# First feed-forward part of a decoder layer: input tiles normed and transposed four at a time, the first weight block split by other engines, the second half's transposes in another place

## The chip, the cores and the metric

The kernel runs on one core of a Trainium2 chip. The time is the device time of one execution in microseconds (us). The engines are PE (TensorE, matrix products), DVE (VectorE), ACT (ScalarE), POOL (GpSimd) and SP (SyncE, which only issues transfers here). Each runs its own row of instructions in order and waits on semaphores for the others.

## The reference

One hybrid decoder layer on x of 1 x 1024 x 1024 in float32. The change concerns the first of its three parts:

```python
x = x + 0.5 * post1(SwiGLU_1(pre1(x)))
# rmsnorm(x, g) = x * rsqrt(mean(x*x) + 1e-6) * g
# swiglu(x)     = (silu(x @ w_gate) * (x @ w_up)) @ w_down     w_gate, w_up: 1024 x 2816
```

Then follow a mixer (stick-breaking attention beside a recurrent head group, between two projections) and a second feed-forward part like the first.

## The kernel before

Every float32 operand of a matrix product is held as two parts, a rounded one (h) and the rest (l), and each product is done as three: h by h, l by h, h by l (`mm3`, lines 119 to 122). `weight` (lines 94 to 110) loads a block of 128 columns of a weight (128 x 1024, 512 KB) into a buffer `wr`, of which there are two, and POOL splits it: line 108 copies it to `wh`, line 109 subtracts for `wl`.

The tokens are worked in two halves of 512. A half's x comes as four tiles of 128 tokens by 1024. Before the change two tiles at a time (`n_00`, `n_01` of the first half, `n_10`, `n_11` of the second) are loaded, squared and summed (ACT line 633, DVE line 768), turned into a factor r by small operations (lines 126 to 137), multiplied by it (ACT line 778, DVE line 780) and given to `to_channels` (line 149). That function transposes on PE (line 159, 128 x 128 each) into a PSUM bank, and from there ACT writes X_0h or X_1h (line 166) and DVE X_0l or X_1l (line 167), channels on partitions. With two tiles a bank holds two blocks of 256 columns, and each is evacuated by itself.

The hidden width has 22 blocks f of 128. Blocks 0 and 1 are plain: `plain_mm(f, h)` does 24 matmuls for the gate (PSUM f1pX) and 24 for the up weight (f1pZ), and `plain_evac` makes silu(gate) * up in a `wr` buffer f1e, splits it and stores it. Blocks 2 to 21 use a form with seven products instead of eight (`product(f)`, in the order 1, 2, 5, 6, 4, 7, 3 into the banks X, Z, DY, X, DW, X, DY, 12 matmuls each). It needs two things: `combine`, sums and differences of X's parts, mostly DVE operations of 128 x 2048 (lines 252 to 267), and `prep(f)`, the same for the raw weights f1r in a scratch f1S of which there is one (DVE lines 303 to 305 and 309), with the split of the seven operands on POOL (lines 314, 315) and ACT (line 312). `load(f)` brings the raw weights, for odd f into the `wr` buffers. `evac1` and `product` read the banks (lines 419 to 449; f1y at line 441, f1v at line 442 and f1u at line 445 are DVE's).

`up` (line 459) runs load(2), combine, plain blocks for the second half, prep(2), and then for each f prep(f+1), load(f+2) and product(f). A scheduler decides the order of each engine's row from the dependencies and its own estimates; the pools decide which buffer must be free first. So the code's order and the rows are not the same, and an edit can move instructions that it does not name.

## Time and profile before

| | us |
|---|---|
| median of 3 runs | 2238.72 |
| lowest and highest | 2233.92, 2238.86 |
| profiled execution | 2238.49 |
| its span, first to last instruction | 2236.7 |
| PE busy | 2106.6 (94%) |
| DVE busy | 1336.3 (60%) |
| POOL busy | 1113.9 (50%) |
| ACT busy | 821.3 (37%) |

PE's mean granted clock is 0.967 of full. The chain that ended last belongs to PE for 76% of the span. A row of the timeline reads: start, duration, engine, line, operation, what it writes and reads, count, and in brackets how long the engine stood idle ahead of it and what released it. Everything that the change names lies in the first 100 us of the 2237.

### The profile page before, as it was taken

What the parts mean: (1) busy time and instruction counts of PE and PEld (TensorE: products, weight loads), DVE (VectorE), ACT (ScalarE), POOL (GpSimd) and SP (SyncE); (2) the same over time, 40 slices, a digit from 0 to 9 for tenths busy, and PEclk for the clock granted to TensorE, in tenths of its full rate; (3) what the DMA queues carried; (4) which work ended last, traced back from release to release, by engine and by line L of the source; (5) the groups of instructions that cost most, each with busy time, mean ns of one, the idle gap of its engine ahead of it and who ended that gap; (6) DMA issues with size and microseconds to landing.
All of it is one profiled execution on the core that took longest, in us unless ns stands there. A gap on an engine that the chain in (4) does not pass through costs nothing.

```text
span 2236.7 us, 30262 instructions
## 1 busy us (share of the span) xinstructions
PE 2106.6 (94%) x10976; PEld 1730.0 (77%) x10976; DVE 1336.3 (60%) x1900; ACT 821.3 (37%) x1429; POOL 1113.9 (50%) x899
## 2 busy tenths in 40 slices
PE   7889999998999999999999999898889999998998
PEld 5668888887888777677888888677668888886886
DVE  5757676742556555735617778636676777733555
ACT  4323333333204534324136657436333333333102
POOL 2676666648742354344311111221687666647734
PEclk8889999999999999999989999999899999998999
DMA  4135555567764463363764673343235554666865
GB/s 123 44 95 165 144 154 149 159 193 282 258 213 132 123 183 119 95 177 98 228 163 118 189 206 115 133 132 131 60 104 158 139 166 131 169 215 212 253 213 188
DMA packets 415476, 353.83 MB, mean 158 GB/s; under 512 B 35168, under 2 KB 337248, under 8 KB 415328
## 3 DMA queue, kind: packets, MB, share of 16 engines
q1 hardware_dynamic: 406800, 347.45, 51.6%
q10 hardware_dynamic: 8528, 4.46, 0.9%
q8 instruction: 87, 1.43, 0.3%
q14 instruction: 61, 0.50, 0.1%
HBM read 224.96 MB, written 126.88 MB: 157 GB/s over the span
## 4 chain that ended last, share of the span: by engine, by line
PE 76%; DVE 9%; issue 4%; POOL 4%; ACT 3%; DMA 2%; SPq 0%; DVEq 0%; POOLq 0%; ACTq 0%
PE pj L120 3%; PE pj L122 3%; PE pj L121 2%; PE f1X L120 2%; PE f2X L120 2%; PE f1X L122 2%; PE f1X L121 2%; PE f2X L122 2%; PE f2X L121 2%; PE f1DY L120 2%; PE f2DY L121 2%; PE f2DY L122 2%; PE f1DY L122 2%; PE f1DY L121 2%; PE f2DY L120 1%
## 5 line engine op out<-in xcount | busy, mean ns | idle before, releaser
L108 POOL TENSOR_SCALAR wh<-wr 128x1024 fp32r<-128x1024 f32 x55 | 62.9, 1145 | 274.6 <-PE wod L122 57.1
L315 POOL TENSOR_TENSOR f1wl<-f1r,f1wh 128x512 fp32r<-128x512 f32 x100 | 139.3, 1406 | 13.0 <-ACT f1wh L312 9.7
L315 POOL TENSOR_TENSOR f2wl<-f2r,f2wh 128x512 fp32r<-128x512 f32 x100 | 139.1, 1404 | 13.0 <-ACT f2wh L312 9.7
L109 POOL TENSOR_TENSOR wl<-wr,wh 128x1024 fp32r<-128x1024 f32 x55 | 137.5, 2503 | 3.2 <-PE pj L122 0.2
L314 POOL TENSOR_SCALAR f1wh<-f1r 128x512 fp32r<-128x512 f32 x60 | 68.0, 1139 | 119.6 <-PE f1pX L121 48.4
L314 POOL TENSOR_SCALAR f2wh<-f2r 128x512 fp32r<-128x512 f32 x60 | 68.0, 1138 | 110.5 <-PE f2pX L121 40.9
L507 DVE TENSOR_TENSOR f2acc<-f2dX,f2acc 128x512 f32<-128x512 f32 x64 | 44.3, 692 | 76.6 <-PE f2dX L122 42.7
L507 DVE TENSOR_TENSOR f1acc<-f1dX,f1acc 128x512 f32<-128x512 f32 x64 | 44.3, 692 | 75.2 <-PE f1dX L122 75.2
L1402 POOL TENSOR_SCALAR a_0B<-a_512B 128x1 f32<-128x1 f32 x32 | 15.4, 481 | 132.0 <-DVE a_512B L1403 98.4
L120 PE MATMUL pj<-x1X4h,wh 128*128 128x512 f32 x176 | 75.5, 429 | 0.5 <-DVE tw L918 0.5
L120 PE MATMUL pj<-x1X2h,wh 128*128 128x512 f32 x176 | 72.1, 409 | 0.6 <-DVE qkl L1113 0.5
L122 PE MATMUL pj<-x1X4h,wl 128*128 128x512 f32 x176 | 71.3, 405 | 0.0
L121 PE MATMUL pj<-x1X4l,wh 128*128 128x512 f32 x176 | 69.7, 396 | 0.0
L122 PE MATMUL pj<-x1X2h,wl 128*128 128x512 f32 x176 | 69.0, 392 | 0.0
L121 PE MATMUL pj<-x1X2l,wh 128*128 128x512 f32 x176 | 68.9, 391 | 0.0
L315 POOL TENSOR_TENSOR f2wl<-f2S,f2wh 128x512 fp32r<-128x512 f32 x40 | 62.3, 1568 | 1.7
L315 POOL TENSOR_TENSOR f1wl<-f1S,f1wh 128x512 fp32r<-128x512 f32 x40 | 62.3, 1568 | 1.7
L533 POOL TENSOR_TENSOR f1dwl<-f1B,f1dwh 128x1024 fp32r<-128x1024 f32 x20 | 47.7, 2412 | 18.9 <-ACT f1dwh L532 18.9
L533 POOL TENSOR_TENSOR f2dwl<-f2B,f2dwh 128x1024 fp32r<-128x1024 f32 x20 | 47.5, 2395 | 19.0 <-ACT f2dwh L532 19.0
L120 PE MATMUL wod<-wh,ymh 128*128 128x512 f32 x128 | 51.1, 399 | 1.1 <-DVE woacc L192 0.9
L122 PE MATMUL wod<-wh,yml 128*128 128x512 f32 x128 | 50.2, 395 | 0.1
L121 PE MATMUL wod<-wl,ymh 128*128 128x512 f32 x128 | 50.1, 392 | 0.0
(1476 smaller groups left out, 7131.6 us busy)
## 6 DMA issues: line engine op xcount, KB each, us to landing
f1ho<-f1hs_d SPq DMA_DIRECT2D x112, 256.0 KB, 4.6
f2ho<-f2hs_d SPq DMA_DIRECT2D x112, 256.0 KB, 4.1
f1hs_d<-f1h SPq DMA_DIRECT2D x56, 256.0 KB, 3.3
f1hs_d<-f1l SPq DMA_DIRECT2D x56, 256.0 KB, 3.0
f2hs_d<-f2h SPq DMA_DIRECT2D x56, 256.0 KB, 3.2
f2hs_d<-f2l SPq DMA_DIRECT2D x56, 256.0 KB, 2.9
wr<-in_w_in_dram SPq DMA_DIRECT2D x27, 512.0 KB, 3.9
f1r<-in_ffn_w_gate_dram SPq DMA_DIRECT2D x19, 512.0 KB, 4.9
```

The source lines that it names most:

```text
L108: nc.gpsimd.tensor_scalar(wh, raw, 1.0, 0.0, op0=ALU.mult, op1=ALU.add)
L109: nc.gpsimd.tensor_tensor(wl, raw, wh, op=ALU.subtract)
L120: nc.tensor.matmul(ps, lhsT=lh, rhs=rh, start=first, stop=False, **kw)
L121: nc.tensor.matmul(ps, lhsT=lh, rhs=rl, start=False, stop=False, **kw)
L122: nc.tensor.matmul(ps, lhsT=ll, rhs=rh, start=False, stop=last, **kw)
L314: nc.gpsimd.tensor_scalar(wh, src[n], 1.0, 0.0, op0=ALU.mult, op1=ALU.add)
L315: nc.gpsimd.tensor_tensor(wl, src[n], wh, op=ALU.subtract)
L507: nc.vector.tensor_tensor(quarter(tt, n), ps, quarter(tt, n), op=ALU.add)
L533: nc.gpsimd.tensor_tensor(wl, src[n], wh, op=ALU.subtract)
L1402: nc.gpsimd.tensor_scalar(B[:, w:w + 1], iv, 1.0, 0.0, op0=ALU.mult, op1=ALU.add)
```

## The change

All four tiles of a half are now loaded by `x_load` and normed together by `x_norm`: one factor r for four tiles, then eight groups of four transposes, each filling a bank of 512 columns that one ACT and one DVE operation evacuate. The first half's banks come from two pools in turn ("D" and "Z"). The gate weight of block 0 is split by ACT (copy) and DVE (subtract) instead of POOL. In the code the second half's loading now stands ahead of both plain blocks, and its norming and transposes between `plain_mm(0, 0)` and `plain_mm(1, 0)`, instead of all of it behind both. The number of matmuls, transposes and warm-up matmuls is the same.

```diff
--- before.py
+++ after.py
@@ -91,7 +91,7 @@
     EX = [None]
     warmt = [None]
 
-    def weight(src, a_, b_, extra=None):
+    def weight(src, a_, b_, extra=None, early=False):
         i = cnt[0]
         cnt[0] += 1
         if extra is None:
@@ -105,8 +105,12 @@
         nc.sync.dma_start(raw, src)
         wh = cut(wp.tile("wh", f"wh{i}", [P, 1024], F32R))
         wl = cut(wp.tile("wl", f"wl{i}", [P, 1024], F32R))
-        nc.gpsimd.tensor_scalar(wh, raw, 1.0, 0.0, op0=ALU.mult, op1=ALU.add)
-        nc.gpsimd.tensor_tensor(wl, raw, wh, op=ALU.subtract)
+        if early:
+            nc.scalar.copy(wh, raw)
+            nc.vector.tensor_tensor(wl, raw, wh, op=ALU.subtract)
+        else:
+            nc.gpsimd.tensor_scalar(wh, raw, 1.0, 0.0, op0=ALU.mult, op1=ALU.add)
+            nc.gpsimd.tensor_tensor(wl, raw, wh, op=ALU.subtract)
         return wh, wl
 
     wz = cp.tile([P, HT], BF16, name="wz")
@@ -327,9 +331,9 @@
             return ps
 
 
-        def plain_load(self, f):
+        def plain_load(self, f, early=False):
             c = slice(f * P, (f + 1) * P)
-            self.op[f] = weight(self.wg[:, :, c], KB, P, False) + weight(self.wu[:, :, c], KB, P, False)
+            self.op[f] = weight(self.wg[:, :, c], KB, P, False, early) + weight(self.wu[:, :, c], KB, P, False)
 
         def plain_mm(self, f, h):
             if f not in self.op:
@@ -753,37 +757,40 @@
     XP[0] = Pool("xp1", XB, "right")
     F1.X = [xpair(f"X1_{h}") for h in range(2)]
     pl = Pool("f1x", dict(t4=8, t2=4))
-    for h in range(2):
-        for p2 in range(2):
-            nm = f"n1_{h}{p2}"
-            xts = []
-            ss = ts(nm + "s", 2)
-            for i in range(2):
-                tt = h * 4 + p2 * 2 + i
-                xt = pl.t4(f"x0_{tt}")
-                nc.sync.dma_start(xt, a["x"][0, tt * P:(tt + 1) * P, :])
-                xts.append(xt)
-                if tt % 2:
-                    junk = pl.t2(f"{nm}j{i}", [P, 1024], BF16)
-                    nc.vector.scalar_tensor_tensor(junk, xt, 1.0, xt, op0=ALU.mult, op1=ALU.mult,
-                                                   accum_out=ss[:, i:i + 1])
-                else:
-                    sumsq_into(pl, f"{nm}q{i}", xt, ss[:, i:i + 1])
-            if h == 0:
-                F1.plain_load(p2)
-            r = rsqrt_col(nm, ss, 1.0 / D, EPS, n=2)
-            for i in range(2):
-                tt = h * 4 + p2 * 2 + i
-                if i == 0:
-                    nc.scalar.activation(xts[i], xts[i], AF.Copy, scale=r[:, i:i + 1])
-                else:
-                    nc.vector.tensor_scalar(xts[i], xts[i], r[:, i:i + 1], 0.0, op0=ALU.mult, op1=ALU.add)
-            if h == 1:
-                warmt[0] = None
-            to_channels(nm, xts, g1, F1.X[h], p2 * 2)
-        if h == 0:
-            F1.plain_mm(0, 0)
-            F1.plain_mm(1, 0)
+    def x_load(h):
+        xts = [pl.t4(f"x0_{h}{i}") for i in range(4)]
+        for i, xt in enumerate(xts):
+            nc.sync.dma_start(xt, a["x"][0, (h * 4 + i) * P:(h * 4 + i + 1) * P, :])
+        return xts
+
+    def x_norm(h, xts):
+        nm = f"n1_{h}"
+        ss = ts(nm + "s", 4)
+        for i, xt in enumerate(xts):
+            if i % 2:
+                junk = pl.t2(f"{nm}j{i}", [P, 1024], BF16)
+                nc.vector.scalar_tensor_tensor(junk, xt, 1.0, xt, op0=ALU.mult, op1=ALU.mult,
+                                               accum_out=ss[:, i:i + 1])
+            else:
+                sumsq_into(pl, f"{nm}q{i}", xt, ss[:, i:i + 1])
+        r = rsqrt_col(nm, ss, 1.0 / D, EPS, n=4)
+        for i, xt in enumerate(xts):
+            if i % 2:
+                nc.vector.tensor_scalar(xt, xt, r[:, i:i + 1], 0.0, op0=ALU.mult, op1=ALU.add)
+            else:
+                nc.scalar.activation(xt, xt, AF.Copy, scale=r[:, i:i + 1])
+
+    x0 = x_load(0)
+    F1.plain_load(0, True)
+    x_norm(0, x0)
+    to_channels("n1_0", x0, g1, F1.X[0], 0, ("D", "Z"))
+    x1 = x_load(1)
+    F1.plain_load(1)
+    F1.plain_mm(0, 0)
+    x_norm(1, x1)
+    warmt[0] = None
+    to_channels("n1_1", x1, g1, F1.X[1], 0)
+    F1.plain_mm(1, 0)
     pl.close()
     F1.up()
     F1.close_x()
```

The lines behind the edit are moved by 4. In the rows below, names of tiles are followed by numbers.

SP's row of loads at the start. x_0 to x_7 before, and x_00 to x_03 and x_10 to x_13 after, are the eight tiles of x; wr is a plain weight block. Before:

```order
L764 DMA x_0_134<-in_x_dram 128x1024
L764 DMA x_1_138<-in_x_dram 128x1024
L105 DMA wr_142<-in_ffn_w_gate_dram 128x8x128
L105 DMA wr_148<-in_ffn_w_up_dram 128x8x128
L764 DMA x_2_209<-in_x_dram 128x1024
L764 DMA x_3_213<-in_x_dram 128x1024
L105 DMA wr_217<-in_ffn_w_gate_dram 128x8x128
L105 DMA wr_223<-in_ffn_w_up_dram 128x8x128
L764 DMA x_4_384<-in_x_dram 128x1024
L764 DMA x_5_388<-in_x_dram 128x1024
```

After:

```order
L763 DMA x_00_133<-in_x_dram 128x1024
L763 DMA x_01_134<-in_x_dram 128x1024
L763 DMA x_02_135<-in_x_dram 128x1024
L763 DMA x_03_136<-in_x_dram 128x1024
L105 DMA wr_141<-in_ffn_w_gate_dram 128x8x128
L105 DMA wr_147<-in_ffn_w_up_dram 128x8x128
L763 DMA x_10_242<-in_x_dram 128x1024
L763 DMA x_11_243<-in_x_dram 128x1024
L763 DMA x_12_244<-in_x_dram 128x1024
L763 DMA x_13_245<-in_x_dram 128x1024
```

The first half's four tiles now stand ahead of both weight blocks of f = 0, and the second half's four ahead of those of f = 1.

PE's row around the end of the plain blocks' first half. n_10p and n_1p are banks of the second half's transposes, f1pZ and f1pX those of plain block f = 1. Before, the last matmuls of block (1, 0) and the first transposes behind them:

```order
L120 MATMUL f1pZ1_0_358<-X1_0h_126,wh3_225 128x512
L121 MATMUL f1pZ1_0_358<-X1_0l_127,wh3_225 128x512
L122 MATMUL f1pZ1_0_358<-X1_0h_126,wl3_226 128x512
L159 MATMUL n1_10p0_406<-ident_60,x0_4_384 128x128
L159 MATMUL n1_10p0_406<-ident_60,x0_5_388 128x128
...
L159 MATMUL n1_10p2_415<-ident_60,x0_4_384 128x128
L159 MATMUL n1_10p2_415<-ident_60,x0_5_388 128x128
```

After, within block (1, 0):

```order
L125 MATMUL f1pX1_0_393<-X1_0l_127,wh2_252 128x512
L126 MATMUL f1pX1_0_393<-X1_0h_126,wl2_253 128x512
L124 MATMUL f1pX1_0_393<-X1_0h_126,wh2_252 128x512
L125 MATMUL f1pX1_0_393<-X1_0l_127,wh2_252 128x512
L163 MATMUL n1_1p2_351<-ident_60,x0_10_242 128x128
L163 MATMUL n1_1p2_351<-ident_60,x0_11_243 128x128
L163 MATMUL n1_1p2_351<-ident_60,x0_12_244 128x128
L163 MATMUL n1_1p2_351<-ident_60,x0_13_245 128x128
L126 MATMUL f1pX1_0_393<-X1_0h_126,wl2_253 128x512
L124 MATMUL f1pX1_0_393<-X1_0h_126,wh2_252 128x512
```

The second half's transposes stood behind all matmuls of the plain blocks (0, 0) and (1, 0); now they stand in groups of four between the matmuls of (1, 0).

DVE's row around the first two products. f1S_705 and f1S_647 are the scratch of block 3, f1S_838 and f1S_780 that of block 4; f1y, f1v and f1u with the banks f1X, f1DW and f1DY are the evacuations of product(2). Before:

```order
L420 TENSOR_TENSOR f1p2_760<-f1Z2_747,f1p2_760 128x512
L441 TENSOR_TENSOR f1y2_777<-f1X2_734,f1y2_777 128x512
L442 TENSOR_TENSOR f1v2_818<-f1DW2_793,f1v2_818 128x512
L303 TENSOR_TENSOR f1S3_705<-f1r1_3_703 128x512
L445 TENSOR_TENSOR f1u2_791<-f1DY2_764,f1u2_791 128x512
L304 TENSOR_TENSOR f1S3_705<-f1S3_705,f1r0_3_701 128x512
L305 TENSOR_TENSOR f1r1_3_703<-f1r0_3_701,f1r1_3_703 128x512
L309 TENSOR_TENSOR f1r0_3_701<-f1r0_3_701,f1S3_705 128x512
L448 TENSOR_TENSOR f1v2_818<-f1p2_760,f1v2_818 128x512
L449 TENSOR_TENSOR f1y2_777<-f1u2_791,f1y2_777 128x512
L303 TENSOR_TENSOR f1S4_838<-f1r1_4_732 128x512
```

After:

```order
L424 TENSOR_TENSOR f1p2_702<-f1Z2_689,f1p2_702 128x512
L307 TENSOR_TENSOR f1S3_647<-f1r1_3_645 128x512
L308 TENSOR_TENSOR f1S3_647<-f1S3_647,f1r0_3_643 128x512
L309 TENSOR_TENSOR f1r1_3_645<-f1r0_3_643,f1r1_3_645 128x512
L313 TENSOR_TENSOR f1r0_3_643<-f1r0_3_643,f1S3_647 128x512
L307 TENSOR_TENSOR f1S4_780<-f1r1_4_674 128x512
L308 TENSOR_TENSOR f1S4_780<-f1S4_780,f1r0_4_672 128x512
L309 TENSOR_TENSOR f1r1_4_674<-f1r0_4_672,f1r1_4_674 128x512
L445 TENSOR_TENSOR f1y2_719<-f1X2_676,f1y2_719 128x512
L446 TENSOR_TENSOR f1v2_760<-f1DW2_735,f1v2_760 128x512
L313 TENSOR_TENSOR f1r0_4_672<-f1r0_4_672,f1S4_780 128x512
L449 TENSOR_TENSOR f1u2_733<-f1DY2_706,f1u2_733 128x512
```

Before, the evacuations f1y and f1v of product(2) stood ahead of the preparation of block 3; now they stand behind all of it and behind three of the four operations for block 4, of which the first writes the one scratch.

## Rows read from the trace of the kernel before

**Rows 1.** Windows, 160 to 450: engines' busy time (count), PE clock, DMA share, GB/s.

```profile
160.00:450.00 290.00, 290.00 (x1279) 239.28 (x1278) 213.35 (x239) 105.54 (x192) 196.39 (x167) 1.00 0.55 152
```

**Rows 2.** Windows, same columns, three stretches behind a stop of PE.

```profile
95.00:101.00 6.00, 5.87 (x14) 4.20 (x15) 3.57 (x4) 1.38 (x3) 5.92 (x5) 0.54 0.00 0
121.30:127.80 6.50, 6.37 (x14) 4.59 (x15) 5.50 (x6) 2.90 (x5) 6.42 (x5) 0.50 0.00 1
142.80:148.40 5.60, 5.60 (x14) 4.45 (x15) 3.95 (x3) 0.12 (x1) 5.52 (x6) 0.51 0.14 42
```

**Rows 3.** Timeline of PE: start, us, engine, line, operation, out<-in, count [idle <-releaser].

```profile
30.07 0.76 PE L120 MATMUL f1pX<-X_0h,wh 128*128 128x512 f32 x1
...
54.13 1.03 PE L159 MATMUL n_10p<-ident,x 128*128 128x128 f32 x8
...
57.40 1.27 PE L159 MATMUL n_10p<-ident,x 128*128 128x128 f32 x8 [2.24 <-DVE X_1l L167]
...
60.23 1.94 PE L159 MATMUL n_11p<-ident,x 128*128 128x128 f32 x8 [1.57 <-DVE X_1l L167]
...
66.70 0.49 PE L122 MATMUL f1pX<-X_1h,wl 128*128 128x512 f32 x1
...
86.57 0.39 PE L122 MATMUL f1pZ<-X_1h,wl 128*128 128x512 f32 x1
...
94.86 0.80 PE L120 MATMUL f1X<-X_0h,f1wh 128*128 128x512 f32 x1 [7.90 <-POOL f1wh L314]
...
121.26 0.79 PE L120 MATMUL f1X<-X_0h,f1wh 128*128 128x512 f32 x1 [4.11 <-POOL f1wh L314]
...
142.75 0.80 PE L120 MATMUL f1X<-X_1h,f1wh 128*128 128x512 f32 x1 [4.28 <-ACT f1u L435]
...
150.93 0.39 PE L120 MATMUL f1X<-X_0h,f1wh 128*128 128x512 f32 x1
```

**Rows 4.** Timeline of DVE, ACT and POOL, the start of the kernel.

```profile
8.20 1.23 DVE L768 SCALAR_TENSOR_TENSOR n_00j<-x 128x1024 bf16<-128x1024 f32 x1 [7.01 <-DMA x<-in_x_dram]
...
14.56 2.94 DVE L780 TENSOR_SCALAR x<-x,n_00r 128x1024 f32<-128x1024 f32 x1
...
19.00 0.48 DVE L167 SCALAR_TENSOR_TENSOR X_0l<-n_00p,g,X_0h 128x256 fp32r<-128x256 f32 x1 [1.50 <-ACT X_0h L166]
...
27.32 0.75 DVE L780 TENSOR_SCALAR x<-x,n_01r 128x1024 f32<-128x1024 f32 x1
...
19.35 0.47 ACT L166 ACTIVATE X_0h<-n_00p,g 128x256 fp32r<-128x256 f32 x1 [0.38 <-PE n_00p L159]
...
10.04 1.04 POOL L108 TENSOR_SCALAR wh<-wr 128x1024 fp32r<-128x1024 f32 x1 [8.68 <-DMA wr<-in_ffn_w_gate_dram]
```

**Rows 5.** Timeline of DVE and POOL, end of the combine, and f1wh of block 2.

```profile
90.84 2.28 DVE L252 TENSOR_TENSOR f1L<-f1R,f1H 128x2048 fp32r<-128x2048 f32 x1
...
73.68 21.13 POOL L314 TENSOR_SCALAR f1wh<-f1r 128x512 fp32r<-128x512 f32 x1 [48.37 <-PE f1pX L121]
```

**Rows 6.** Timeline of POOL and DVE, preparation of blocks 3 and 4.

```profile
120.59 0.62 POOL L314 TENSOR_SCALAR f1wh<-f1r 128x512 fp32r<-128x512 f32 x1 [11.70 <-DMA f1r<-in_ffn_w_gate_dram]
...
129.62 1.06 POOL L314 TENSOR_SCALAR f1wh<-f1r 128x512 fp32r<-128x512 f32 x1
...
130.65 1.29 POOL L315 TENSOR_TENSOR f1wl<-f1S,f1wh 128x512 fp32r<-128x512 f32 x1
...
116.61 0.68 DVE L442 TENSOR_TENSOR f1v<-f1DW,f1v 128x512 f32<-128x512 f32 x1
...
122.30 0.81 DVE L303 TENSOR_TENSOR f1S<-f1r 128x512 f32<-128x512 f32 x1 [5.01 <-DMA f1r<-in_ffn_w_up_dram]
...
131.98 1.75 DVE L303 TENSOR_TENSOR f1S<-f1r 128x512 f32<-128x512 f32 x1 [1.78 <-POOL f1wl L315]
...
133.77 0.98 DVE L304 TENSOR_TENSOR f1S<-f1S,f1r 128x512 f32<-128x512 f32 x1
...
134.68 1.77 DVE L305 TENSOR_TENSOR f1r<-f1r,f1r 128x512 f32<-128x512 f32 x1
```

## The prediction

> **What bounds the kernel now.** I read four views, in this order. First the table of windows, to see where TensorE (PE) is the limit: from 160 to 450 us it is busy all the time, at full clock [rows 1]. Whatever the change does to the first 150 us, that stretch can only be pushed to the left or right. One matmul there takes 290 us / 1279 = 0.227 us. The same table by narrow stretches shows where PE is slow [rows 2]: from 95 to 101, 121.3 to 127.8 and 142.8 to 148.4 the granted clock is 0.50 to 0.54, the 1.2 GHz level, and a matmul takes 6.37/14 = 0.455 us, twice as much. Second, PE's own rows show a stop ahead of each of these three, and what ended it [rows 3]: first matmul at 30.07, the second half's transposes only at 54.13, in groups that wait 2.24 and 1.57 us for the evacuations, the plain blocks over at 86.57 + 0.39 = 86.96, then 7.90 us for POOL's f1wh, 4.11 us for the next f1wh, 4.28 us for the ScalarE copy f1u. Third, the start on VectorE (DVE), ScalarE (ACT) and GpSimd (POOL) [rows 4]. Fourth, DVE and POOL around 73 and 116 to 132 us, which is where the stops come from [rows 5, 6].
>
> So the bound of the first 151 us is a chain: x landed, normed, transposed, plain blocks, combined second half, first product, second product. After 150.93, when block f4's first matmul starts, PE has its weights in time. I forecast by moving that 150.93.
>
> **Step 1, until the first matmul.** Removed: two rounds of norming become one; 16 evacuations of 128x256 per half and engine become 8 of 128x512; the second round's transposes no longer wait behind the first round's evacuation. Added: all four tiles must have landed, and the gate block's split now takes an ACT copy and a DVE subtract. The third 512 KB block landed at 10.04, 1.84 us behind the second at 8.20 [rows 4]. Now the third and fourth blocks are x, so x_03 is there at 10.04 + 1.84 = 11.9, and the gate block at 13.7. Behind the last x stand a square-sum of 1.23 and the small ops. Before, the way from 8.20 to the last norming multiply's start at 14.56 took 6.4 us with POOL's split running beside it; undisturbed I put it at 3.0, so r is there at 14.9. Bounds 14.9 and 18.3. Then on DVE x_01, the new subtract, x_03. The multiply took 0.75 undisturbed and 2.94 beside POOL's subtract [rows 4]; the subtract on DVE of a 128x1024 pair is half of a 128x2048 one, 2.28/2 = 1.14 [rows 5]. Undisturbed sum 0.75 + 1.14 + 0.75 = 2.6, so x_03 is ready at 17.5; with the up block's split on POOL in the way, up to 2.94 - 0.75 = 2.2 more, twice over at worst, 21.9. I take 19, between, since POOL gets the up block only at about 15.6. Five groups of four transposes stand before the first matmul; cold, eight took 1.94 [rows 3], so 20 take 4.9: first matmul at **24.0**, against 30.07. Bounds 22.4 and 26.8. The Trainium skill ("SBUF — State Buffer", "Who interferes with whom") has a rule that speaks against moving the split to DVE: an operation with two SBUF inputs and a GpSimd operation that reads SBUF exclude each other, and whoever comes second waits. The 2.94 us row bears it out for this place; by that rule alone the start would be 26.8, by undisturbed rows 22.4.
>
> **Step 2, the plain blocks.** 192 matmuls by 0.227 are 43.5 us. 12 transposes of the first half and 32 of the second stand between them at 0.13 each (eight took 1.03 at full clock [rows 3]), 5.7. The first ten matmuls are at the low clock, 10 x 0.23 = 2.3. The sum is 51.5, so the plain blocks end at 24.0 + 51.5 = **75.5**, 11.5 us earlier than 86.96. What was exposed before, the waits of 2.24 and 1.57 and the low clock from 60.23 to 66.70 [rows 3], now lies beside the matmuls of (1,0): between two groups of transposes stand two or three matmuls, 0.45 to 0.7 us, plus the group's 0.52, so a group comes every 1.0 to 1.2 us. An evacuation of 256 columns took 0.47 on ACT and 0.48 on DVE [rows 4]; one of 512 costs at most 0.94 and 0.96, below a group's pace. So this is hidden; if not (up to 0.3 us for each of 8 groups), 2.4 us.
>
> **Step 3, the first product.** It waits for POOL's f1wh, which took 21.13 us for what POOL did in 0.62 at 120.59 [rows 5, 6]: it began at 73.68 and was over when DVE's unbroken row of 128x2048 adds paused. That row has 11 adds, 2.2 us from start to start; so 24.2, and about 3.5 of small pieces stand among them. It can start when the second half is evacuated. The second half starts at 24.0 + 48 x 0.227 + 2.3 + 1.6 = 38.8, and eight groups of 1.0 to 1.3 end at 47 to 49. The row of adds ends at 75 to 77. The price of the PE wait then falls from 7.90 to 0 to 2; I take 0.5, so f1X starts at **76.0** instead of 94.86, and no stop of 4 us or more, the size behind which the low clock came [rows 2, 3], stands ahead of it. The product itself is 84 x 0.227 = 19.0. POOL, whose backlog of f2 weights now starts with the product and not ahead of it, will hold PE for one or two pieces of about 1.3 [rows 6]: 2 us, bounds 0 and 4. End **97.0**; before, f3's first matmul came at 121.26 after a stop of 4.11, so the product ended at 117.15: 20.1 us earlier.
>
> **Step 4, the second product, where something is given back.** Its raw weights (f3) land at 120.6 (gate) and 122.3 (up) [rows 6], behind the stores of the plain results on SP. These stores hang on DVE's splits behind the row of adds, which is about 19 us earlier; gate stands further forward in SP's row than before, ahead of f4's up block. I take gate at 94.7 and up at 98.5. With the old distance from POOL's work instead, 11.7 us behind its end at 76 + 14 [rows 6], gate would come at 101.2 and up at 102.9; that is the other bound. X and Z of f3 (24 matmuls, 5.4) end at 102.4. The third matmul group (DY) must have the bank that f2's evacuations read, and here the scheduler's new order bites: f2's two evacuations, in front of f3's preparation before, now stand behind all of f3's and three adds of f4's. The first add of f4 needs f3's S buffer, which POOL releases last: before, from up landed to that add 131.98 - 122.30 = 9.7 us. One POOL piece of f4 that stood ahead of it (1.06) now stands behind, and up comes 3.8 us behind gate and not 1.7, so that POOL has 2.1 us more of f3 behind it: 9.7 - 1.1 - 2.1 = 6.5. Three adds of 1.75, 0.98 and 1.77 and two evacuations of 0.7 make about 5.9 more [rows 6]. The evacuations are over at 98.5 + 6.5 + 5.9 = 110.9: PE stands still for 8.5 us where two stops of 4.11 and 4.28 were, and has one low-clock stretch, 12 x 0.23 = 2.8, where two were. The five groups left are 60 x 0.227 = 13.6. End 110.9 + 2.8 + 13.6 = **127.3**, against 150.93.
>
> The rest is instruction for instruction the same and bound by PE, so the gain is 150.93 - 127.3 = 23.6 us, and the profiled run's 2238.49 us (span 2236.7 and 1.8 around it) becomes 2214.9; the median is 0.23 above that run, so **2215**.
>
> **Rivals.**
> (a) No stop at DY. If POOL is through with f3's S soon enough, or up lands earlier, PE runs on: 97.0 + 19.0 = 116.0, gain 35, time 2204. Against it: six POOL pieces of 0.6 to 1.3 behind the landing [rows 6].
> (b) The clock. Transposes are mixed with matmuls from the first group to the last. At 60.23 eight transposes, four matmuls and more transposes ran slow until 66.70 [rows 3]; at 54.13, right behind matmuls, eight ran at full rate. If the low level holds from 24 until the second half is through, 58 matmuls cost 0.23 more each, 13 us, 2.3 of it in my sum already: gain 13, time 2226. The Trainium skill ("TensorE: Matmul & The Clock Gate", Part 4) says that a transpose does not count as busy for the clock in the way that a matmul does, which is this case; the trace has a row on either side.
> (c) The loads of f3 don't come earlier. Landed at 122.3 still, f2's evacuations would be over at 134.7, the second product at 151.1: gain 0, time 2238.7. This is the case that the start is won and given back in full. Against it: SP waits there only for stores that come earlier.
> (d) Slower: the preparation falls behind for good. Each time PE stops for a weight it pays the stop and the low clock, 4.28 + 2.8 = 7.1 [rows 2, 3]. With the second product starting 20 us earlier, the lead of the preparation that stood at 150.93 is gone; if DVE's order stops PE in f4 to f8 too, five times 7.1 are 35: loss 12, time 2250. It decides from the fourth stop on. Against it: from 160 on DVE and POOL are busy 74 and 68% of the time while PE runs without a stop [rows 1], so they catch up.
> (e) It doesn't do what it says: the first half waits so long for x_03 and the split that the first matmul is not earlier than 28. Then 4 us of the gain go: 2219, inside the range.
>
> **How the numbers follow.** Forecast with its bounds (2209 to 2220, case (e) in it): 0.55. (a) 0.15, (b) 0.19, (c) 0.06, (d) 0.05. The range of 8 in 10 is 2203 to 2226: it takes the forecast, most of (a) and most of (b). Faster by more than 0.3% (6.7 us, about what a measurement here tells from no change) 0.89, within 0.3% 0.06, slower 0.05.
>
> **What would show it.** Right: first matmul near 24; second-half transposes between matmuls of (1,0) without idle; f1X of f2 near 76 with under 2 us of wait; one stop of PE of 5 to 9 us ahead of f3's DY, put down to DVE's evacuation; f4's X near 127, then PE without a gap. Wrong: a clock near 0.5 from 24 to 50; a stop of over 2 us ahead of f2's product; f3's up landing after 103; stops in f4 or later.

## The result, and the profile after

| | before | after |
|---|---|---|
| median of 4 runs, us | 2238.79 | 2211.52 |
| lowest and highest | 2233.92, 2239.46 | 2210.87, 2215.21 |
| profiled execution, span | 2238.49, 2236.7 | 2211.98, 2210.3 |
| mean granted clock of PE | 0.967 | 0.976 |

The ratio is 0.9886, with a 95% interval of 0.9865 to 0.9906: 1.1% faster, 27.3 us between the medians, 26.4 us between the profiled spans. The forecast was 2215 with a range of 2203 to 2226.

PE's timeline after, in the columns of [rows 3], the rows that answer to them and the stops:

```profile
14.79 1.42 PE L163 MATMUL n_0p<-ident,x 128*128 128x128 f32 x5 [4.10 <-ACT x L781]
...
16.82 3.25 PE L163 MATMUL n_0p<-ident,x 128*128 128x128 f32 x15 [0.61 <-DVE x L779]
...
19.83 0.47 PE L124 MATMUL f1pX<-X_0h,wh 128*128 128x512 f32 x1
...
70.07 0.39 PE L124 MATMUL f1X<-X_0h,f1wh 128*128 128x512 f32 x1
...
71.64 0.50 PE L126 MATMUL f1X<-X_0h,f1wl 128*128 128x512 f32 x1 [0.95 <-POOL f1wl L319]
...
81.16 0.50 PE L126 MATMUL f1X<-f1H,f1wl 128*128 128x512 f32 x1 [1.05 <-POOL f1wl L319]
...
91.36 0.80 PE L124 MATMUL f1X<-X_1h,f1wh 128*128 128x512 f32 x1 [4.92 <-ACT f1u L439]
...
98.51 0.39 PE L124 MATMUL f1X<-X_0h,f1wh 128*128 128x512 f32 x1
...
107.60 0.47 PE L124 MATMUL f1DY<-f1H,f1wh 128*128 128x512 f32 x1 [3.49 <-DVE f1v L446]
...
120.03 0.50 PE L124 MATMUL f1X<-X_1h,f1wh 128*128 128x512 f32 x1 [2.23 <-ACT f1u L439]
...
125.60 0.39 PE L124 MATMUL f1X<-X_0h,f1wh 128*128 128x512 f32 x1
```

The first matmul comes at 19.83 (30.07 before), block f2 starts at 70.07 with no stop ahead of it (94.86 behind a stop of 7.90), f3 at 98.51 (121.26) and f4 at 125.60 (150.93). From there on the order of all engines is the one of before, and PE is busy without a gap again:

```profile
150.00:440.00 290.00, 290.00 (x1279) 239.14 (x1278) 207.41 (x236) 106.30 (x192) 198.12 (x168) 1.00 0.54 150
```

So 25.33 us of the gain are there when f4 starts. The second feed-forward part's first product starts at 1574.58, against 1599.94: 25.36, the same. The other 1.0 us between the spans lies behind that.

The start, in the columns of [rows 4]. DVE, then POOL:

```profile
13.43 0.75 DVE L779 TENSOR_SCALAR x<-x,n_0r 128x1024 f32<-128x1024 f32 x1
...
14.10 1.22 DVE L110 TENSOR_TENSOR wl<-wr,wh 128x1024 fp32r<-128x1024 f32 x1
...
15.24 1.53 DVE L779 TENSOR_SCALAR x<-x,n_0r 128x1024 f32<-128x1024 f32 x1
...
14.26 1.97 POOL L112 TENSOR_SCALAR wh<-wr 128x1024 fp32r<-128x1024 f32 x1 [12.89 <-DMA wr<-in_ffn_w_up_dram]
```

PE's clock there, in the table of windows (columns of [rows 1]):

```profile
16.80:19.80 3.00, 2.98 (x15) 2.98 (x15) 3.00 (x1) 2.29 (x4) 2.18 (x1) 0.51 1.05 362
19.80:22.00 2.20, 1.71 (x13) 1.26 (x12) 2.20 (x6) 2.20 (x5) 0.84 (x1) 1.00 1.06 272
```

And the way from the row of adds to f3, in the columns of [rows 5, 6]. POOL's f1wh and DVE beside its end:

```profile
53.78 15.36 POOL L318 TENSOR_SCALAR f1wh<-f1r 128x512 fp32r<-128x512 f32 x1 [24.72 <-PE f1pX L125]
...
68.57 0.68 DVE L355 TENSOR_TENSOR f1e<-f1pZ,f1e 128x512 f32<-128x512 f32 x1
```

ACT's two copies ahead of f2's last X group, and SP's two loads that answer to the first of them:

```profile
90.21 0.62 ACT L316 CAST f1wh<-f1r 128x512 fp32r<-128x512 f32 x1 [8.49 <-DMA f1r<-in_ffn_w_gate_dram]
...
90.73 0.58 ACT L439 COPY f1u<-f1X 128x512 f32<-128x512 f32 x1
...
82.97 0.37 SPq L285 DMA_DIRECT2D f1r<-in_ffn_w_gate_dram  x1
...
84.08 0.45 SPq L285 DMA_DIRECT2D f1r<-in_ffn_w_gate_dram  x1
```

DVE's first add for f3, its first add for f4, and the evacuation f1v of f2 behind them (its place in [rows 6] was 116.61, ahead of all preparation):

```profile
94.92 0.69 DVE L307 TENSOR_TENSOR f1S<-f1r 128x512 f32<-128x512 f32 x1 [14.35 <-DMA f1r<-in_ffn_w_up_dram]
...
101.80 1.09 DVE L307 TENSOR_TENSOR f1S<-f1r 128x512 f32<-128x512 f32 x1 [2.43 <-POOL f1wl L319]
...
106.78 0.67 DVE L446 TENSOR_TENSOR f1v<-f1DW,f1v 128x512 f32<-128x512 f32 x1
```

### The profile page after: what moved, and what is told of

Its sections match the earlier page's. It is cut to its first block, busy times and chain, and to the rows that moved or that the text cites. A ratio compares the mean times of both kernels' runs of the same rounds, so it can differ in the third digit from the quotient of the medians.

```text
span 2210.3 us, 30206 instructions
## 1 busy us (share of the span) xinstructions
PE 2094.5 (95%) x10976; PEld 1719.9 (78%) x10976; DVE 1329.6 (60%) x1873; ACT 817.2 (37%) x1412; POOL 1108.3 (50%) x897
## 4 chain that ended last, share of the span: by engine, by line
PE 76%; DVE 9%; issue 4%; ACT 4%; POOL 4%; DMA 2%; SPq 0%; DVEq 0%; ACTq 0%; POOLq 0%
PE pj L124 3%; PE pj L126 2%; PE pj L125 2%; PE f2X L124 2%; PE f1X L124 2%; PE f2X L125 2%; PE f2X L126 2%; PE f1X L126 2%; PE f1X L125 2%; PE a_512o L1430 2%; PE f2DY L125 2%; PE f1DY L125 2%; PE f2DY L124 2%; PE f1DY L126 2%; PE f2DY L126 2%
## 5 line engine op out<-in xcount | busy, mean ns | idle before, releaser
L319 POOL TENSOR_TENSOR f1wl<-f1r,f1wh 128x512 fp32r<-128x512 f32 x100 | 141.2, 1424 | 15.9 <-ACT f1wh L316 12.7
L318 POOL TENSOR_SCALAR f1wh<-f1r 128x512 fp32r<-128x512 f32 x60 | 60.0, 1005 | 91.6 <-PE f1X L125 27.0
```

What stands on the lines that cost most here:

```text
L318: nc.gpsimd.tensor_scalar(wh, src[n], 1.0, 0.0, op0=ALU.mult, op1=ALU.add)
L319: nc.gpsimd.tensor_tensor(wl, src[n], wh, op=ALU.subtract)
```

## Experiments

All kernels are the changed kernel with the edits shown, and each is timed against the kernel before on the same chip (medians of before: 2234.99 for experiments 1 to 4, 2235.49 for 5 to 7, 2238.85 for 8 to 10). Experiments 8 and 9 show the edit against the experiment before. Left out of the edits shown are lines that only note an instruction for another to stand behind, branches that stay as they were, and in the third the names and counts for two tiles inside `x_norm`. The totals of one kernel can lie 10 us and more apart, more than some of these edits are worth: the stretch from about 500 us (PE's last stop in the first part) to about 1490 (the transposes of the mixer's result), in which no edit lies, took 987 to 1000 us in the profiled executions. So the edits are compared by the time at which f4's first matmul starts, each in its one profiled execution. Behind that PE runs alike: to its last stop in the first part it takes 369.1 to 370.9 us in all twelve kernels. The kernels whose start carries no edit have their first matmul between 19.83 and 20.72, so a difference of under 1 us says nothing.

| | first matmul | f2 | f3 | f4 | median, us | ratio to before, interval |
|---|---|---|---|---|---|---|
| before | 30.07 | 94.86 | 121.26 | 150.93 | 2238.79 | |
| after | 19.83 | 70.07 | 98.51 | 125.60 | 2211.52 | 0.9886 (0.9865 to 0.9906) |
| undo_split | 24.29 | 74.47 | 104.19 | 132.12 | 2215.25 | 0.9909 (0.9884 to 0.9934) |
| undo_place | 20.07 | 70.48 | 104.47 | 133.08 | 2220.27 | 0.9936 (0.9918 to 0.9954) |
| undo_four | 23.63 | 75.66 | 100.58 | 135.20 | 2227.71 | 0.9965 (0.9950 to 0.9980) |
| act_free | 20.72 | 70.83 | 92.52 | 126.40 | 2213.49 | 0.9898 (0.9874 to 0.9923) |
| sp_f3_first | 20.21 | 70.31 | 91.99 | 118.33 | 2209.59 | 0.9884 (0.9854 to 0.9914) |
| dve_f2_first | 20.04 | 70.17 | 98.04 | 126.39 | 2213.87 | 0.9902 (0.9880 to 0.9925) |
| both | 19.87 | 69.97 | 91.64 | 119.70 | 2205.76 | 0.9866 (0.9845 to 0.9886) |
| three | 20.01 | 70.13 | 91.80 | 112.06 | 2204.94 | 0.9851 (0.9823 to 0.9878) |
| three_two_parts | 20.37 | 70.44 | 92.16 | 112.38 | 2190.21 | 0.9790 (0.9766 to 0.9814) |
| warm_longer | 18.09 | 71.50 | 99.90 | 126.96 | 2211.14 | 0.9896 (0.9867 to 0.9925) |

**1. The split undone.**

```diff
-    F1.plain_load(0, True)
+    F1.plain_load(0)
```

> The changed kernel, but the gate block of f = 0 is split on POOL as before. Theory (the start is a chain of x landed, normed, transposed, and all later work hangs on it): POOL begins the gate's split at 12.4, in the middle of DVE's small operations, and holds them and the multiply of x_03 as it did before (2.94 us for 0.75), so the first matmul comes about 2 us later than 19.83 and everything to f4's first matmul shifts by that: 125.6 + 2 = 127.6, time about 2213.5 (bounds 0 and 4 us later than the changed kernel). Rival (the split only has to be there before PE wants wl, and POOL has time for it): no shift, 2211.5, with the first matmul at 19.8.

Measured: first matmul at 24.29, 4.5 us later, f4 at 132.12, 6.5 later. DVE and POOL of this kernel:

```profile
12.95 0.91 DVE L134 TENSOR_TENSOR n_0e<-n_0y,n_0m 128x4 f32<-128x4 f32 x1
...
14.09 2.21 DVE L136 TENSOR_SCALAR n_0e<-n_0e 128x4 f32<-128x4 f32 x1
...
17.32 3.61 DVE L779 TENSOR_SCALAR x<-x,n_0r 128x1024 f32<-128x1024 f32 x2
...
13.93 2.34 POOL L113 TENSOR_TENSOR wl<-wr,wh 128x1024 fp32r<-128x1024 f32 x1
```

The theory holds and was sized too small. POOL's subtract of the gate block runs from 13.93 to 16.27, and beside it DVE's small operation on 128 x 4 numbers lasts until 16.30: it took 2.21 us for what takes 0.17 in the changed kernel. Two more of them, beside POOL's copies of the two blocks, took 0.91 and 0.96 for 0.17 and 0.16. Then the two multiplies take 3.61, beside POOL's split of the up block, for 0.75 and 1.53 in the changed kernel. The moved split is worth its 4.5 us at the start (0.3 of them are a later landing of x_03, 10.94 and not 10.62), not for the weights' sake but because it takes POOL out of the way of DVE's norm. The remaining 2 us come in f2, which takes 29.7 us instead of 28.4, and in f3, 27.9 instead of 27.1.

**2. The place undone.**

```diff
+    F1.plain_mm(1, 0)
     x_norm(1, x1)
     warmt[0] = None
     to_channels("n1_1", x1, g1, F1.X[1], 0)
-    F1.plain_mm(1, 0)
```

> The changed kernel, but the second half is normed and transposed behind both plain blocks of the first half, as before. Theory (the place is the largest part, since it sets when the second half is complete and so when DVE's row of eleven adds ends): the second half is complete at about 53 and not 44.8, the adds end about 8 us later, PE stops 2 to 4 us for POOL's f1wh and runs at the low clock behind it, f4's first matmul at 131 to 136, time 2217 to 2222. Rival (the adds have slack, and what counts is the earlier first matmul): the whole shift is under 3 us, 2211.5 to 2214.

Measured: f4 at 133.08, inside the theory's 131 to 136, but not by its steps. Three stops of PE, and DVE's f1v:

```profile
81.67 0.77 PE L124 MATMUL f1DW<-f1H,f1wh 128*128 128x512 f32 x1 [2.87 <-ACT f1H L253]
...
104.47 0.79 PE L124 MATMUL f1X<-X_0h,f1wh 128*128 128x512 f32 x1 [5.73 <-POOL f1wh L318]
...
125.97 0.79 PE L124 MATMUL f1X<-X_1h,f1wh 128*128 128x512 f32 x1 [4.98 <-ACT f1u L439]
...
98.19 0.68 DVE L446 TENSOR_TENSOR f1v<-f1DW,f1v 128x512 f32<-128x512 f32 x1
```

f2 starts at 70.48, as early as in the changed kernel: PE fills the time with plain matmuls, and the transposes go between those of (0, 1) and (1, 1). What is later is the combine, whose results f1H and f1L PE now awaits inside f2 (2.87 and 1.62), and with it POOL's work, the stores and f3's loads (stops of 5.73 and 4.98). The place is worth 7.5 us, paid in f2 and f3 and not ahead of f2. Here DVE's f1v stands at 98.19, ahead of f3's preparation as before: the scheduler's new order in DVE's row comes with the new place, and the 7.5 us are what the two are worth together.

**3. Two tiles at a time.**

```diff
-    x_norm(0, x0)
-    to_channels("n1_0", x0, g1, F1.X[0], 0, ("D", "Z"))
+    for p2 in range(2):
+        x_norm(0, x0[2 * p2:2 * p2 + 2], p2)
+        to_channels(f"n1_0{p2}", x0[2 * p2:2 * p2 + 2], g1, F1.X[0], p2 * 2, ("D", "Z"))
...
-    x_norm(1, x1)
-    to_channels("n1_1", x1, g1, F1.X[1], 0)
+    for p2 in range(2):
+        x_norm(1, x1[2 * p2:2 * p2 + 2], p2)
+        to_channels(f"n1_1{p2}", x1[2 * p2:2 * p2 + 2], g1, F1.X[1], p2 * 2)
```

> The changed kernel, but each half is normed, transposed and evacuated two tiles at a time (two factors r, 16 evacuations of 256 columns on each engine). Loads, split and place stay. Theory: the first half is complete about 3 us later, since DVE's small operations come twice and the second pair stands behind the first pair's evacuations; the second half's evacuations cost 0.48 x 2 instead of 0.69 a group and hold PE a little; f4's first matmul 2 to 5 us later, time 2213.5 to 2216.5. Rival (two tiles can begin earlier, at the landing of the second, and win what they lose): within 1 us of the changed kernel.

Measured: f4 at 135.20, 9.6 later, twice the theory's 2 to 5. DVE's subtract for the gate block, and PE:

```profile
16.11 3.36 DVE L110 TENSOR_TENSOR wl<-wr,wh 128x1024 fp32r<-128x1024 f32 x1
...
17.03 0.66 PE L163 MATMUL n_01p<-ident,x 128*128 128x128 f32 x4 [2.60 <-ACT x L781]
...
21.18 2.79 PE L163 MATMUL n_01p<-ident,x 128*128 128x128 f32 x12 [3.50 <-DVE X_0l L171]
...
127.36 0.79 PE L124 MATMUL f1X<-X_1h,f1wh 128*128 128x512 f32 x1 [10.57 <-ACT f1u L439]
```

The first pair does begin earlier, its transposes at 12.49, and loses it: the second pair waits 2.60 for its multiply and 3.50 for the first pair's evacuations, and these stand on DVE behind the subtract for the gate block, which took 3.36 us beside POOL's subtract for the up block instead of 1.22. The first matmul is 3.8 later, f2 is 5.6 later, and in f3 a stop of 10.57 stands ahead of the last X group, by the same chain on ACT and DVE as in the seventh experiment. Here too DVE's row is another one: f2's f1y and f1v stand ahead of f4's adds (106.77 and 111.02). So the part that I had counted as two rounds of norming and some evacuations carries the largest share, but in part because it lets the moved subtract run ahead of POOL's. By the medians it costs about 16 us (the nine totals of this kernel are 2224.87 to 2232.94); the order of all engines behind f4 is the same, and why more than the 9.6 is lost there is open.

The three parts undone one by one cost 6.5, 7.5 and 9.6 us, 23.6 together, of the 25.3 that the change gains there. None of them is idle. That they nearly add up does not show that they act apart, since undoing the second and the third also changed the order of DVE's row.

**4. The stop ahead of f2's last X group, which the prediction did not have.**

```diff
-                if n in (2, 6, 7):
+                if n in (2, 6, 7) and not (f == 3 and n == 2 and self.nm == "f1"):
                     nc.scalar.copy(wh, src[n])
```

> The changed kernel, but one cast of block f3 (the second operand, from the gate's raw weights) is done by POOL instead of ACT, so that ACT's copy f1u of f2 no longer stands behind a cast that waits for f3's gate to land. Theory (two stops in a row share one cause, the late landing of f3): the stop of 4.92 us ahead of f2's last X group and its low clock go, but DY of f3 still waits for DVE's f1v at about 107.5, so that stop grows from 3.5 to 8 to 9 us; f4's first matmul moves by under 2.5 us either way, time 2209.5 to 2213. Rival (each stop is a cost of its own): f4's first matmul 6.5 us earlier, time 2205.

Measured: f3 at 92.52, 6.0 earlier, and f4 at 126.40, 0.8 later (the start, which this edit leaves alone, came 0.9 later here). PE:

```profile
108.41 0.76 PE L124 MATMUL f1DY<-f1H,f1wh 128*128 128x512 f32 x1 [9.34 <-DVE f1v L446]
```

The stop of 4.92 is gone and the one ahead of f3's DY has grown from 3.49 to 9.34. In ACT's row the copy f1u stood behind the cast that waited 8.49 us for f3's gate; taking that away only moves the waiting. Both stops have one cause further back, as the theory had it; the next experiment shows which.

**5. f3's loads ahead of f4's on SP.**

```diff
+                if f == 4 and self.nm == "f1":
+                    with tc.issue_after(self.late):
+                        nc.sync.dma_start(t, w[:, :, c])
+                else:
+                    d = (nc.scalar if f == 2 else nc.sync).dma_start(t, w[:, :, c])
+                    if f == 3 and self.nm == "f1":
+                        self.late = d.ins
```

> The changed kernel, but on SP the two loads of f4's raw weights are issued behind the two of f3's, in the first part only. Theory (f3's gate lands at 90.2 because its issue at 84.1 stands in SP's row behind f4's gate, which waits until 83.0 for a buffer of f2): gate lands at about 84.5 and up at about 89; the stop of 4.92 us ahead of f2's last X group goes with its low clock, and f2's evacuations behind f3's and f4's adds are over at about 101 instead of 107.5; f4's first matmul at about 119, time 2205. Rival (the buffers of f3 are free only when the stores of the plain results have landed, whatever the order): landings within 1.5 us of before, time within 1.5 us of 2211.5.

Measured: f4 at 118.33, 7.3 earlier than in the changed kernel. SP, ACT and PE:

```profile
77.63 0.37 SPq L289 DMA_DIRECT2D f1r<-in_ffn_w_gate_dram  x1
...
81.77 0.62 ACT L322 CAST f1wh<-f1r 128x512 fp32r<-128x512 f32 x1 [0.26 <-DMA f1r<-in_ffn_w_gate_dram]
...
100.22 0.77 PE L124 MATMUL f1DY<-f1H,f1wh 128*128 128x512 f32 x1 [2.63 <-DVE f1v L452]
```

f3's gate is issued at 77.63 instead of 84.08 and is there at 81.8 instead of 90.2. ACT's cast hardly waits (0.26), the stop of 4.92 is gone, and the one ahead of DY is 2.63. f3's up is issued at 82.60 instead of 90.94. This is the cause: a load that could go stood in SP's row behind one for f4, which waited until 82.97 for a buffer that POOL still read (SP's queue waits 7.5 us there for POOL's f1wl of f2). f3's up waited for a store of a plain result, and that store stood behind the same load. The median is only 1.9 us lower, and the ratio to before (0.9884) is that of the changed kernel: the totals of this kernel run from 2203.84 to 2216.89, and the profiled execution is the longest. In it PE's granted clock between 1200 and 1300 us was 0.85, in the changed kernel's 0.98.

**6. f2's evacuations ahead of f4's preparation on DVE.**

```diff
+            if f == 4 and self.nm == "f1":
+                with tc.issue_after(self.ev):      # ev: the add that makes f1v of f2
+                    tt(S1, A21, A22, op=ALU.add)
```

> The changed kernel, but on DVE the first add of f4's preparation is issued behind f2's evacuations f1y and f1v, in the first part only. Theory (the stop ahead of f3's DY is DVE's order and nothing else): f1v is over at about 100.7 instead of 107.45, the stop of 3.49 us and the low clock behind it go, f4's preparation is some 1.4 us later; f4's first matmul about 4 to 5 us earlier, at 121, time 2207. Rival (the stop is only moved to the next bank or to f4's weights, since the late landing of f3 delays all preparation): f4's first matmul within 1.5 us of 125.6 or stops of the same sum behind it.

Measured: f4 at 126.39, 0.8 later: the theory fell, the rival holds. PE:

```profile
119.39 0.79 PE L124 MATMUL f1X<-X_1h,f1wh 128*128 128x512 f32 x1 [6.64 <-ACT f1u L443]
```

The stop ahead of DY is gone, and one of 6.64 has come ahead of f3's last X group.

**7. Both.**

```diff
+                if f == 4 and self.nm == "f1":
+                    with tc.issue_after(self.late):
+                        nc.sync.dma_start(t, w[:, :, c])
...
+            if f == 4 and self.nm == "f1":
+                with tc.issue_after(self.ev):
+                    tt(S1, A21, A22, op=ALU.add)
```

> Both edits in one, the loads of f3 first on SP and f2's evacuations ahead of f4's adds on DVE, in the first part only. Theory: no stop of over 2.5 us is left between the first matmul and f4; f4's first matmul at 110 to 114, time 2196 to 2200. Rival (the preparation of f4 and f5 becomes the bound, POOL and DVE together): a new stop in f4 or f5 eats more than half of it, time 2203 to 2208.

Measured: f4 at 119.70, 1.4 later than with the loads' order alone, median 2205.76. The theory of no stop over 2.5 us fell; the new stop is in f3 itself, not in f4 or f5, where the rival had it; the time is in the rival's range. DVE, ACT and PE:

```profile
105.98 1.09 DVE L317 TENSOR_TENSOR f1S<-f1r 128x512 f32<-128x512 f32 x1 [2.42 <-POOL f1wl L329]
...
109.26 0.68 DVE L434 TENSOR_TENSOR f1p<-f1Z,f1p 128x512 f32<-128x512 f32 x1
...
109.97 0.63 ACT L435 ACTIVATE f1p<-f1p 128x512 f32<-128x512 f32 x1 [10.19 <-DVE f1p L434]
...
111.49 0.59 ACT L449 COPY f1u<-f1X 128x512 f32<-128x512 f32 x1
...
112.13 0.80 PE L124 MATMUL f1X<-X_1h,f1wh 128*128 128x512 f32 x1 [6.53 <-ACT f1u L449]
```

The chain reads backwards: PE waits for ACT's copy f1u (111.49), which stands behind the activation of f1p (109.97), which needs DVE's add f1p (109.26), and that stands in DVE's row behind f5's three adds, of which the first waited for POOL until 105.98. Z of f3 had been complete at about 97.

**8. The add f1p of f3 ahead of f5's preparation too.**

```diff
-            if f == 4 and self.nm == "f1":
-                with tc.issue_after(self.ev):
+            if f in (4, 5) and self.nm == "f1":
+                with tc.issue_after(self.ev if f == 4 else self.ep):      # ep: the add f1p of f3
```

> As the run with both edits, and in DVE's row the add f1p of f3 now also stands ahead of f5's first preparation add (first part only). Theory (the stop of 6.53 us that was left ahead of f3's last X group comes from ACT's copy f1u, which stands behind the activation of f1p, which waits for DVE's f1p behind f5's adds, and these wait for POOL): the add f1p is done at about 100 instead of 109.9, ACT's copy at about 101, and PE runs from 20 us to f4 without a stop of over 1.1 us; f4's first matmul at 111 to 113 instead of 119.7, time about 2198. Rival (PE then runs into f4's or f5's weights): a new stop of 3 us or more in f4 or f5, f4's first matmul at 111 to 113 but f6's not more than 4 us ahead of the run with both edits.

Measured: f4 at 112.06, 13.5 us earlier than in the changed kernel. PE:

```profile
106.49 0.50 PE L124 MATMUL f1X<-X_1h,f1wh 128*128 128x512 f32 x1 [0.77 <-ACT f1u L451]
```

All stops between 21 and 112 us are now 1.03 us or less, and from 60 to 112 us the granted clock is 1.00. In f5 one of 1.12 is left, so f6 starts 12.2 us earlier than in the changed kernel (151.55 against 163.75) and 6.3 earlier than with both edits: the theory holds at f4 and f6, the rival fell. The time of about 2198 did not come: the median is 6.6 us lower than the changed kernel's, with totals from 2197.39 to 2206.99. Whether the second edit is needed beside the other two was not run.

**9. The same order in the second part.**

```diff
-                if f == 4 and self.nm == "f1":
+                if f == 4:
...
-                    if f == 3 and self.nm == "f1":
+                    if f == 3:
...
-            if f in (4, 5) and self.nm == "f1":
+            if f in (4, 5):
```

> The same three edits of order in the second feed-forward part too, whose start is otherwise as in the kernel before. Theory: there the stop of 8 us ahead of f2's first matmul comes from DVE's row of adds against POOL and stays, but the stops ahead of f3's first X group (2.9 and 0.6) and ahead of f3's last X group (3.9, behind f1u's counterpart) go with their low clock; 5 to 9 us less than with the edits in the first part alone, time about 2191. Rival (in the second part f3's weights come late for another reason than SP's order): within 2 us of it.

Measured: median 2190.21, ratio 0.979 (0.9766 to 0.9814), the best of all. PE in the second part, first without the edits there (experiment 8), then with them; the first matmul of f2, the stops ahead of f3 and in f3:

```profile
1568.88 0.79 PE L124 MATMUL f2X<-x2X2h,f2wh 128*128 128x512 f32 x1 [7.90 <-POOL f2wh L328]
...
1593.65 0.50 PE L124 MATMUL f2X<-x2X2h,f2wh 128*128 128x512 f32 x1 [2.46 <-POOL f2wh L328]
...
1615.14 0.58 PE L124 MATMUL f2X<-x2X4h,f2wh 128*128 128x512 f32 x1 [5.03 <-ACT f2u L451]
```

```profile
1561.97 0.80 PE L124 MATMUL f2X<-x2X2h,f2wh 128*128 128x512 f32 x1 [7.87 <-POOL f2wh L328]
...
1601.34 0.50 PE L124 MATMUL f2X<-x2X4h,f2wh 128*128 128x512 f32 x1 [3.38 <-ACT f2u L451]
```

From f2's first matmul to the one ahead of which PE stops in f3 it is 46.26 us without and 39.37 with the edits: 6.9 us less, inside the 5 to 9. The stops ahead of f3 are gone, of the one in f3 3.38 are left: there DVE's add f2p stands behind the last operation for f4, which waits for POOL until 1597.46. The two profiled executions are 15.9 us apart. Of the 9.0 beyond the 6.9, again 6.9 lie ahead of the second part (f2 there starts at 1561.97 and 1568.88), in the stretch that varies, and the rest behind f4 there. So the edits account for 6.9 of the 14.7 us between the medians, and that the time of about 2191 was met is in part luck.

**10. More idle matmuls ahead of the transposes.**

```diff
-    warm(24)
+    warm(41)
```

> The changed kernel with 17 more of the idle matmuls that stand ahead of the first transposes (49 instead of 32), so that PE is busy until about 14.6 and not 10.7. Theory (the first 20 transposes run at the low clock level because PE stood still for 4.1 us ahead of them, and only the evacuations hold them otherwise): the transposes take 0.13 each, the first matmul comes 1 to 1.5 us earlier, near 18.5, f4's first matmul 0.5 to 1.5 us earlier, time about 2210.5. Rival (the evacuation on DVE, which begins only at 20.0 behind a square-sum of the second half, sets the pace): first transposes faster, but second matmul at 21.2 as before and f4 within 0.5 us of 125.6.

Measured: first matmul at 18.09, f4 at 126.96, 1.4 later. DVE and PE:

```profile
16.91 3.31 DVE L772 SCALAR_TENSOR_TENSOR n_1j<-x 128x1024 bf16<-128x1024 f32 x1
...
14.94 1.39 PE L163 MATMUL n_0p<-ident,x 128*128 128x128 f32 x11 [1.45 <-ACT x L781]
...
20.95 0.76 PE L163 MATMUL n_0p<-ident,x 128*128 128x128 f32 x4 [2.36 <-DVE X_0l L171]
...
21.94 0.63 PE L126 MATMUL f1pX<-X_0h,wl 128*128 128x512 f32 x1
```

The transposes ran at full clock, 0.13 each. But then PE waited 2.36 us for DVE's evacuation, which begins at about 20 whatever PE does. It stands behind a square-sum of the second half, which takes 3.3 us in both kernels, beside POOL's subtract of the up block, where the one at 8.03 took 1.23. Behind that wait the granted clock was 0.61 from 20.9 to 23.0, and the third matmul took 0.63 where it had taken 0.40. The theory fell. The rival was right that DVE sets the pace; that the faster transposes would cost 1.4 us at f4, by the pause that they open, neither had.

## Why the prediction was right, and where it was not

At f4 the gain was 25.33 us and the forecast 23.6. On the way it stood at 24.8 at f2 and 22.8 at f3, where the forecast had 18.9 and 24.3: something was given back, for the reason that I gave, f3's weights, but it was paid in f2 and not in f3, which took 27.1 us against 29.7 in the kernel before. Point by point:

- **Step 1, wrong in size.** First matmul at 19.83, forecast 24.0, bounds 22.4 to 26.8. The term that failed is the cover for POOL: I took 19 for x_03, since POOL's split of the up block would hold DVE. It held it once, for 0.78 us (the multiply at 15.24 took 1.53 and not 0.75), and x_03 was ready at 16.77. Also r was there at 13.4 and not 14.9, x_03 having landed at 10.6. (The bound of 18.3 that I gave for r is not in the bound of 26.8.) The 24.0 that I forecast is close to what the kernel does with the split left on POOL (24.29): I had counted the move as a subtract more on DVE, and not that it takes POOL's gate split away from DVE's small operations. The rule of the Trainium skill that I weighed ("SBUF — State Buffer", "Who interferes with whom"), for operations with two SBUF inputs, agrees with experiment 1, where two such operations took 0.91 and 0.96 us and ended with POOL's copies; but it spoke for this edit more than against it. My row of 2.94 us does not bear it out, nor does the 2.21: both are operations with one tensor as input, which the rule as I put it does not cover.
- **Step 1, second term.** The transposes ahead of the first matmul ran at the low clock, as forecast (15 in 3.25 us). But 5 of the 20 were done before x_03 was ready, so the term was 3.1 and not 4.9. From 19.8 on the granted clock was 1.00, so the ten slow matmuls in step 2 never came.
- **Step 2, right.** From the first matmul to f2 it took 50.24 us, forecast 51.5; without the 2.3 for slow matmuls 49.2. The second half was complete at 44.8, and no stop is left there.
- **Step 3, right in its main part.** POOL's f1wh began at 53.78, took 15.36 and ended at 69.14, before PE asked at 70.07. Two stops of 0.95 and 1.05 for pieces of f1wl are the 2 us of the sum. **Missed: the stop of 4.92 ahead of the last X group and the low clock behind it.** I had read DVE's row for f2 and f3, and not ACT's, where f3's cast stands ahead of f2's copy. The product took 28.4 us, forecast 21.0; f3 started at 98.51, forecast 97.0, although f2 had started 5.9 earlier than I forecast.
- **Step 4, right in where it stops, not in size, nor in what held the loads.** f3's gate and up came at 90.2 and 94.9, forecast 94.7 and 98.5 and so below both my bounds. I had them hang on the stores behind the row of adds. What held SP was the load of f4's gate, until POOL had read f2's gate for the last time (82.95), with the last two stores and f3's gate behind it, as experiment 5 shows. POOL was through with all of f2 at 84.19, where I had it 14 us behind f2's start, at 90. f1v was over at 107.45, forecast 110.9. The stop ahead of DY was 3.49 and not 8.5, since f3 had started late: the stop that I had missed took its place in part, which is why missing it cost the forecast little. Experiment 4 shows it: without the first stop the second is 9.34. A further stop of 2.23 ahead of f3's last X group was missed too.
- **The rivals.** (a), no stop at DY, is what experiment 8 builds: 112.06. (b), the low clock among the transposes, did not come; the granted clock is 1.00 from 19.8 to 90. (c) did not come: the loads are 27 to 30 us earlier. (d) did not come: PE has no stop from 125.60 to 440. (e) neither.

So the number was right by errors that nearly cancel: f2 started 5.9 us earlier than I had it, its product took 7.4 more, for a stop with its low clock that I had not seen, and f3 took 3.2 less. That 1.7 us are left of these is in part luck. Of the prediction's own signs f4's X near 127 came (125.60); the first matmul near 24, f2 near 76 and a stop of 5 to 9 us at DY came as 19.83, 70.07 and 3.49.

## What to carry to other kernels

An operation moved off an engine can pay through its neighbour: the split of one weight block was worth 4.5 us at the start because POOL's copy and subtract no longer stood beside DVE's smallest operations. When a start is pulled forward, read every engine's row of what follows for instructions that wait at its head for something that has not moved, the queue that issues loads among them: here one on SP and two on DVE, with ACT passing their waits on, cost 13.5 us. They hid each other: moving the waiting out of ACT's or DVE's way alone gave nothing (experiments 4 and 6), the late load alone gave half (5), and all three together gave the whole (8).

## What the runs showed of the hardware

In the changed kernel PE's clock rose while PE did nothing but transposes: 20 of them, from 14.79 to 19.8, with no matmul between, and the granted clock went from 0.51 to 1.00 just ahead of the first matmul. The Trainium skill ("TensorE: Matmul & The Clock Gate", Part 4) says that a transpose does not count as busy in the way that a matmul does; this stretch differs from that, if the transposes here run in the mode that the page means, which the rows don't show.

The rise does not come at this point every time. With the split undone (experiment 1) the clock was still 0.50 behind 20 transposes, the last 19 without a pause, until 26.4, and with three edits (experiment 8) it was 0.64 from 19.8 to 22.0. In the kernel before, the transposes came in groups of eight with pauses of 3 to 4 us; the granted clock was 0.50 from 16 to 32 us, and the first matmul behind them still ran slow [rows 3]. The last group was

```profile
28.30 1.97 PE L159 MATMUL n_01p<-ident,x 128*128 128x128 f32 x8 [3.84 <-ACT x L778]
```

POOL's f1wh of 128 x 512, asked for at 53.78, ended at 69.14. DVE's operations around its end each read two operands from SBUF, but for the one at 68.57, which reads one from PSUM; 68.57 + 0.62 (the length of that POOL operation when nothing else runs) is 69.19. So by these times it was held for the whole row of adds and went through beside the one operation that reads PSUM, and not at the end of the row (70.46), as I had put it. In the kernel before the row had no such operation until its end at 94.33, and f1wh was over at 94.81. The Trainium skill ("SBUF — State Buffer", "Who interferes with whom") says that an operation of DVE with at most one SBUF input, outside the modes in which it uses two ports, leaves GpSimd alone; these rows agree.
